# A hybrid state-space and delta-rule trunk layer on one core: the delta rule run as three side lines, state-space batches with prefetched inputs and a doubling recurrence, and the conditioning vectors loaded at other times

## The chip, the core and the metric

The kernel runs on one core of a Trainium2 chip. The metric is the time of one execution on the device in microseconds (us). Before the change the median of three runs is 3185.92 us (3182.63 to 3190.62).

## The reference, cut to what matters

One layer over 512 tokens of width 2048. A conditioning vector `c` gives six modulation vectors of 2048 entries each through the 2048 x 12288 matrix `w_ada`.

```python
mod = silu(c) @ w_ada + b_ada                       # six vectors
sh_m, sc_m, g_m, sh_f, sc_f, g_f = split(mod, 6)
h = layer_norm(x) * (1 + sc_m) + sh_m
u, q, k, v, z, beta, a, gate_s, gate_g = split(h @ w_in)
y_s = s5_mixer(u) @ w_up_ssm        # 64 groups, diagonal complex recurrence, GLU
y_g = gated_deltanet(q, k, v, z, beta, a) @ w_up_gdn      # 8 heads, chunks of 64
y = (sigmoid(gate_s) * y_s + sigmoid(gate_g) * y_g) @ w_out
x = layer_norm(ALPHA * x + g_m * y)
h = layer_norm(x) * (1 + sc_f) + sh_f
x = layer_norm(ALPHA * x + g_f * swiglu(h))
```

In the state-space mixer each group's state follows x[t] = A x[t-1] + B u[t] with a diagonal complex A. In the delta rule each head needs, for each chunk, the inverse of a unit lower triangular matrix, and then a recurrence over the chunks that updates a 128 x 128 state.

## The kernel before, in words

**The large products.** Every matrix of weights is cut into chunks of 128 x 1024 numbers (512 KB), numbered here from 0 in the order of use. Class `Weights` (L886) loads a chunk through SyncE's queue into `raw`, ScalarE copies it to `whi` (a cast to fp32r), VectorE subtracts to get the rest `wlo`, and TensorE takes both: three matmuls (`mm3`) for each 128 x 128 block. `raw`, `whi` and `wlo` have three buffers each (`NB = 3`). A chunk feeds 24 matmuls of 512 columns where the weights stand still in the array (`gemm1`, `gemm2`), but only 12 of 512 columns in the output projection (the loop over `hf` and `q` behind `ln_half`), since that runs over the weights twice, once for each half of the tokens. Chunks 0 to 17 are the projection to u and to beta and a; 18 to 145 the 16 pairs of gate columns and, for each of 8 heads, q, k, v and z; 146 to 153 the GLU; 154 to 185 the two up-projections that are merged; 186 to 249 the output projection. From 250 on it is the feed-forward network, whose first eight hidden tiles are taken over the first half of the tokens (chunks 250 to 281) and then over the second.

**Side lines.** All else is written as generators (lines) that class `Order` (L57) mixes into the matmuls when the kernel is built: it keeps an estimated clock for each engine and lets a line emit its next step where its inputs should be ready (`tick`), or, in `until`, runs lines without any large matmul between until a condition holds. The result is one fixed order for each engine, and each engine works in order.

- *State space* (`s5_setup`, `s5_batch`, `s5_line`): eight batches of eight groups. A batch loads U, B and C through SyncE, builds tables of powers on GpSimd (`powers`), does small matmuls, then runs the recurrence on VectorE as 7 steps over 64 columns and 7 steps over 8 columns (`cstep`, four operations each), a correction on GpSimd, more matmuls, GELU, and a store.
- *Delta rule* (`gdn_prep`, `gdn_solve` and the lines that call them): one line prepares head h (decays, products of keys), the other inverts the triangular blocks in five levels and runs the recurrence over four double chunks. The output of the recurrence, `po`, is held in one of the three accumulators of the large products (`psum_mm`). The preparing line starts head h when head h-2 is done.
- *Conditioning vectors* (`ada_line`, `ada_cols_line`, `ada_row_line`): each vector of 2048 is made in four parts of 512. A part is 16 loads of 128 x 512 numbers of `w_ada` (256 KB each), each scaled and added into `aacc`. Before the change these loads go through GpSimd's queue, and 5 of every 16 are scaled on ScalarE and added on GpSimd, the others on VectorE. sh_m and sc_m are made ahead of everything. The other four, 16 parts, are line `ada_rest` (L1350), added by `switch` when state space and delta rule are done.

**Who needs the vectors.** g_m is needed by the output projection (`k.ada_m`). sh_f and sc_f are needed by `ln_half`, which normalizes one half of the tokens, transposes it on TensorE (`px_tr<-cst,ld`) and writes the inputs of the feed-forward network; it waits in `while not k.ada_f`. `ln_half(0)` must be finished (`o.drain(lnl)`) before the feed-forward network starts, and `ln_half(1)` before its second half of tokens. g_f is needed behind the first group of hidden tiles (`k.ada_done`).

Of the kernel before, what the change touches and what calls it, by code (L numbers as in the profile page):

```python
# [11 lines left out]
F32 = mybir.dt.float32  # L12
# [259 lines left out]
def s5_setup(k, p, lam_re, lam_im, log_dt):  # L272
# [8 lines left out]
    s.R8s = per.tile([128, 2, 32], F32, name="R8s")  # L281
    s.R64s = per.tile([128, 2, 32], F32, name="R64s")
# [85 lines left out]
    for dst, i in ((s.R8s, 0), (s.R64s, 7)):  # L368
        e.tensor_scalar(out=dst[:, 0, :], in0=R[:, 1, i, :], scalar1=-1.0, scalar2=None, op0=M)
        e.tensor_copy(out=dst[:, 1, :], in_=R[:, 1, i, :])  # L370


def s5_batch(k, j, prm, d_col):
# [5 lines left out]
    U = t("U")  # L379
    ld.dma_start(out=U.rearrange("p (g c) -> p g c", g=8),  # L380
                 in_=k.dup[j].rearrange("(g h) (s c) -> (h s) g c", g=8, s=8))
    B = k.sm5.tile([128, 2, 8, 16], F32, name="s5B", tag="s5B")
    for half in range(2):
        for sw in range(2):
            src = (b_re, b_im)[half ^ sw]
            ld.dma_start(out=B[64 * half:64 * half + 64, sw], in_=src[0, g0:g0 + 8].rearrange("g p h -> p g h"))
    Cin = k.sm5.tile([128, 3, 64], F32, name="s5C", tag="s5C")
    for i, src in enumerate((c_re, c_im, c_re)):
        ld.dma_start(out=Cin[:, i, :], in_=src[0, g0:g0 + 8].rearrange("g h p -> (g h) p"))
# [20 lines left out]
    H = k.t5w("H").rearrange("p (g h s) -> p g h s", g=8, s=8)  # L410
# [37 lines left out]
    St = t("S").rearrange("p (q r b i) -> p q r b i", q=4, r=2, b=8)  # L448
    pSv = pS.rearrange("p (g b i) -> p g b i", g=8, b=8)
    for gp in range(2):  # L450
        for ri in range(2):
            act.copy(St[64 * gp:64 * gp + 64, :, ri].rearrange("p q b i -> p q (b i)"),
                     pSv[64 * ri:64 * ri + 64, gp::2].rearrange("p g b i -> p g (b i)"))
    yield
# [4 lines left out]
    q0 = 4 * j  # L459
    w1 = k.sm5.tile([128, 4, 2, 8], F32, name="s5w1", tag="s5w1")  # L460

    def cstep(dst, prev, rr, rs, n):
        x = w1[:, :, :, 0:n]
        shp = [128, 4, 2, n]
        for src, cf_ in ((prev, bc(rr.unsqueeze(2).unsqueeze(3), shp)), (prev[:, :, ::-1], bc(rs.rearrange("p r q -> p q r").unsqueeze(3), shp))):
            v.tensor_tensor(out=x, in0=src, in1=cf_, op=M)
            v.tensor_tensor(out=dst, in0=dst, in1=x, op=A)
    a8r, a8s = s.R8[:, 0, 0, q0:q0 + 4], s.R8s[:, :, q0:q0 + 4]
    a64r, a64s = s.R8[:, 0, 7, q0:q0 + 4], s.R64s[:, :, q0:q0 + 4]
    for i in range(1, 8):  # L470
        cstep(St[:, :, :, :, i], St[:, :, :, :, i - 1], a8r, a8s, 8)
        if i % 2 == 0:
            yield
    for b in range(1, 8):
        cstep(St[:, :, :, b, 7:8], St[:, :, :, b - 1, 7:8], a64r, a64s, 1)
        if b % 3 == 0:
            yield
    yield R
    Tp = k.t5w("K").rearrange("p (g n) -> p g n", g=8)
    act.copy(Tp.rearrange("p g (h s) -> p g s h", s=8), R.rearrange("p g (s h) -> p g s h", s=8))  # L480
    yield
    wf = k.sm5.tile([128, 4, 7, 7], F32, name="s5wf", tag="s5wf")
# [10 lines left out]
    pool.memset(X[:, :, 0:1], 0.0)  # L493
    for gp in range(2):
        for ri in range(2):
            act.copy(X[64 * ri:64 * ri + 64, gp::2, 1:64],
                     St[64 * gp:64 * gp + 64, :, ri].rearrange("p q b i -> p q (b i)")[:, :, 0:63])
    powers(H, C, slice(1, 9), S)
    yield
# [28 lines left out]
def gdn_setup(k, p, psb, a_log, dt_bias, conv_w, norm_w):  # L528
# [13 lines left out]
    s.TT = per.tile([128, 512], F32, name="TTfull")  # L542
    pool.memset(s.TT, 0.0)
# [203 lines left out]
def gdn_solve(k, h, r):  # L747

    v, act, pool, pe = k.v, k.act, k.pool, k.pe
    s, t = k.gd, k.tg  # L750
# [6 lines left out]
    def col(nm):  # L757
        return k.sm.tile([128, 4], F32, name=nm, tag="gd" + nm, bufs=2)
# [27 lines left out]
    for i in range(2):  # L786
        p = slice(64 * i, 64 * i + 64)
        v.tensor_copy(out=v4(s.TT)[p, :, p], in_=v4(TT)[p])
# [3 lines left out]
    v.tensor_scalar(out=v4(s.TT)[0:64, :, 64:128], in0=v4(px[:, 0:256])[0:64], scalar1=-1.0, scalar2=None, op0=M)  # L792
    TT = s.TT
# [19 lines left out]
    po = k.psum_mm()  # L813
    for n in T4:
        pvn = k.psum("gd")
        pe.matmul(pvn[:, 0:128], lhsT=n_(TT, n), rhs=n_(bv, n), start=True, stop=(n == 0))
        if n:
            pe.matmul(pvn[:, 0:128], lhsT=n_(wT, n), rhs=St, start=False, stop=True)
            pe.matmul(n_(po, n), lhsT=n_(r.qd, n), rhs=St, start=True, stop=False)
# [5 lines left out]
        pe.matmul(n_(po, n), lhsT=n_(r.ET, n), rhs=vn, start=(n == 0), stop=True)  # L825
# [6 lines left out]
    yield po  # L832
    so, ro = col("so"), col("ro")
    junk = t("th")
    for n in T4:
        act.activation(n_(junk, n), n_(po, n), AF.Square, accum_out=so[:, n:n + 1])
# [5 lines left out]
    on = t("th")  # L842
    v.tensor_tensor(out=v4(on), in0=v4(po), in1=c4(ro), op=M)
# [25 lines left out]
def gdn_solve_line(k):  # L869
    for h in range(8):  # L870
        while k.heads_ready <= h:
            yield 1.0
        yield from gdn_solve(k, h, k.prepped.pop(h))
# [88 lines left out]
def kernel(ctx, tc, x, c, w_ada, b_ada, w_in, lam_re, lam_im, log_dt, b_re, b_im, c_re, c_im,  # L962
# [828 lines left out]
```

## Time and profile before

| | |
|---|---|
| median of three runs | 3185.92 us |
| profiled execution, its own time | 3192.52 us |
| its span, first to last instruction | 3190.7 us |
| TensorE busy | 3039.6 us, 95% of the span |
| VectorE, ScalarE, GpSimd busy | 1649.5, 976.4, 879.7 us |
| moved from and to HBM | 458.17 MB |

The profile gives each engine's busy time, by window of time too, with the clock that TensorE was granted, the busy share of the 16 DMA engines and their GB/s. "Waits" name who waited for whom. "Groups" collect instructions by line, engine and tiles: busy us and mean ns of one, then idle time of the engine just before them and what ended it. "The chain" follows the work that ended last back from its end. Almost everything carries L170 or L211, the helpers that record an operation, so one reads by tile names; `w` is a load of `w_ada`, `s_` are state-space tiles, `g_` and `px_gd` delta-rule tiles, `at` and `bt` are activations, `pm` and `px_fo` accumulators of the large products.

### The profile page before, as it was taken

The page shows a single profiled execution, that of the slowest core. Times are in us where ns is not written, and L with a number is a line of the kernel's source. Part 1 is how long each engine was busy: PE and PEld are TensorE (multiplying, and loading weights), DVE is VectorE, ACT ScalarE, POOL GpSimd, SP SyncE. Part 2 cuts the span into 40 slices and gives each one's busy share as a digit, 9 for nine tenths or more (in the row PEclk, how much of TensorE's full clock was granted, in tenths as well). Part 3 has the DMA queues.
Part 4 walks back from the last instruction along what each step waited for, and adds up shares of the span by engine and source line. Part 5 has one row for each costly group of instructions (what it writes and reads, how often), then busy time and mean ns, then how long its engine had stood idle before and what let it go on. Part 6 is the DMA issues. An engine that isn't in the chain of part 4 may idle for free.

```text
span 3190.7 us, 40575 instructions
## 1 busy us (share of the span) xinstructions
PE 3039.6 (95%) x15953; PEld 2507.5 (79%) x15953; DVE 1649.5 (52%) x2407; ACT 976.4 (31%) x1386; POOL 879.7 (28%) x997
## 2 busy tenths in 40 slices
PE   5899999999999999998878899999999999999997
PEld 3588788888788888886758798888888888888885
DVE  6536664566545377767778653333333333333338
ACT  3233333333333244334345531221222222222121
POOL 4824434434352143333344203002001100200202
PEclk8899999999999999999989999999999999999999
DMA  9644233333333488778878463333333333333333
GB/s 339 217 126 109 72 82 92 93 88 81 84 98 86 152 283 267 235 246 290 272 232 242 137 177 108 94 99 111 94 99 108 97 99 104 101 99 97 108 106 119
DMA packets 505344, 458.17 MB, mean 144 GB/s; under 512 B 56144, under 2 KB 403632, under 8 KB 505152
## 3 DMA queue, kind: packets, MB, share of 16 engines
q1 hardware_dynamic: 477472, 375.34, 39.1%
q0 software_dynamic: 20480, 67.13, 6.2%
q10 hardware_dynamic: 7200, 13.10, 1.1%
q8 instruction: 125, 2.05, 0.3%
q14 instruction: 67, 0.55, 0.1%
HBM read 435.60 MB, written 19.89 MB: 143 GB/s over the span
## 4 chain that ended last, share of the span: by engine, by line
PE 78%; DVE 7%; DMA 6%; POOL 3%; issue 3%; ACT 2%; SPq 1%; ACTq 0%; DVEq 0%; POOLq 0%
PE pm L211 56%; PE px_fo L211 14%; PE px_gd L211 3%; DMA raw<-in_w_mix_out_dram 3%; PE px_s L211 2%; DVE wlo L170 2%; DVE at L170 1%; SPq L170 1%; DVE aacc L170 1%; ACT whi L170 1%; DMA w<-in_w_ada_dram 1%; DMA raw<-in_ffn_w_in_dram 1%; PE px_u L211 1%; POOL eq L170 1%; PE px_ada L211 0%
## 5 line engine op out<-in xcount | busy, mean ns | idle before, releaser
L211 PE MATMUL pm<-at,whi 128*128 128x512 f32 (+1 forms) x3744 | 1142.6, 388 | 7.4 <-ACT whi L170 3.6
L170 DVE TENSOR_TENSOR wlo<-raw,whi 128x1024 fp32r<-128x1024 f32 x541 | 698.4, 1293 | 773.2 <-ACT whi L170 761.3
L170 ACT CAST whi<-raw 128x1024 fp32r<-128x1024 f32 x541 | 567.0, 1049 | 1068.0 <-PE pm L211 464.8
L211 PEld LDWEIGHTS pm<-at,whi 128*128 128x128 f32 x3744 | 681.5, 190 | 138.8 <-issue 4.1
L211 PE MATMUL pm<-at,wlo 128*128 128x512 f32 (+1 forms) x1872 | 715.4, 382 | 6.4 <-DVE wlo L170 6.4
L211 PE MATMUL pm<-bt,whi 128*128 128x512 f32 (+1 forms) x2464 | 682.1, 363 | 0.7 <-ACT whi L170 0.7
L211 PEld LDWEIGHTS pm<-bt,whi 128*128 128x128 f32 x2464 | 443.9, 190 | 72.4 <-ACT whi L170 1.1
L211 PE MATMUL pm<-bt,wlo 128*128 128x512 f32 (+1 forms) x1232 | 446.9, 363 | 5.7 <-DVE wlo L170 5.7
L170 POOL TENSOR_TENSOR at<-at,ld 128x512 f32<-128x512 f32 x80 | 120.5, 1537 | 1106.9 <-DVE ld L170 1106.9
L211 PEld LDWEIGHTS pm<-at,wlo 128*128 128x128 f32 x1872 | 355.6, 190 | 76.5 <-DVE wlo L170 8.0
L211 PE MATMUL px_fo<-whi,bt 128*128 128x512 f32 x960 | 298.8, 389 | 0.0
L211 PEld LDWEIGHTS pm<-bt,wlo 128*128 128x128 f32 x1232 | 233.6, 190 | 42.6 <-DVE wlo L170 6.9
L211 PEld LDWEIGHTS px_fo<-whi,bt 128*128 128x128 f32 x960 | 180.1, 188 | 37.4
L170 POOL DMA_DIRECT2D w<-in_w_ada_dram x237 | 128.7, 544 | 291.2 <-DVE aacc L170 178.6
L211 PE MATMUL px_fo<-wlo,bt 128*128 128x512 f32 x480 | 186.7, 389 | 0.0
L170 DVE SCALAR_TENSOR_TENSOR aacc<-w,ccol,aacc 128x512 f32<-128x512 f32 x148 | 135.6, 916 | 13.4 <-DMA w<-in_w_ada_dram 11.8
L211 PE MATMUL pm<-whi,bt 128*128 128x512 f32 x336 | 112.2, 404 | 13.1 <-DVE at L170 13.0
L170 POOL TENSOR_TENSOR aacc<-aacc,w 128x512 f32<-128x512 f32 x59 | 88.2, 1495 | 77.9 <-ACT w L170 77.4
L211 PE MATMUL px_fo<-whi,at 128*128 128x512 f32 x336 | 107.5, 389 | 1.7 <-ACT whi L170 1.7
L211 PEld LDWEIGHTS px_fo<-wlo,bt 128*128 128x128 f32 x480 | 90.1, 188 | 18.7
L170 DVE SCALAR_TENSOR_TENSOR gs<-gg,pm 128x512 f32<-128x512 f32 x36 | 24.8, 688 | 142.1 <-ACT gg L170 142.1
L211 PEld LDWEIGHTS pm<-whi,bt 128*128 128x128 f32 x336 | 65.5, 195 | 30.5 <-DVE at L170 16.0
(389 smaller groups left out, 3173.6 us busy)
## 6 DMA issues: line engine op xcount, KB each, us to landing
raw<-in_ffn_w_in_dram SPq DMA_DIRECT2D x208, 512.0 KB, 4.0
raw<-in_w_in_dram SPq DMA_DIRECT2D x146, 512.0 KB, 3.7
w<-in_w_ada_dram POOLq DMA_DIRECT2D x237, 256.0 KB, 4.6
raw<-in_ffn_w_out_dram SPq DMA_DIRECT2D x88, 512.0 KB, 3.7
wad<-in_w_ada_dram SPq DMA_DIRECT2D x64, 512.0 KB, 5.8
raw<-in_w_mix_out_dram SPq DMA_DIRECT2D x64, 512.0 KB, 5.8
raw<-in_w_up_gdn_dram SPq DMA_DIRECT2D x16, 512.0 KB, 4.0
raw<-in_w_up_ssm_dram SPq DMA_DIRECT2D x16, 512.0 KB
```

The source lines that it names most:

```text
L170: r = f(*a, **kw)
L211: r = self.e.matmul(out, **kw)
```

## The change

1. **Conditioning vectors.** g_m becomes its own line, `ada_gate`, added before the state-space and delta-rule work: its 64 loads go through SyncE's queue, one in at least 6.0 us of the planner's clock (`pace`), and all adding is on VectorE. sh_f and sc_f (128 loads) stay on GpSimd's queue from `switch` on. g_f (64 loads) goes through SyncE at a pace of 3.5 us, on VectorE alone. In the order of the built programs `switch` comes ahead of chunk 118 and no longer of chunk 130. By the chunks that are split on VectorE, the sixteen parts were made from chunk 130 to 276: g_m at 130 to 152, sh_f and sc_f at 154 to 227, g_f at 229 to 276. Now g_m is made at 17 to 106, sh_f and sc_f at 118 to 157, and g_f at 159 to 245. Of g_f's four parts two, 32 loads, stand between chunks 196 and 245, inside the output projection, and none behind it.
2. **State space.** `fetch(j + 1)` loads the inputs of the next batch from the middle of batch j; U has two buffers. The powers `H` come ahead of the recurrence, the loads of `R` behind it. The recurrence is done by doubling: distances 1, 2 and 4, over 448, 384 and 256 columns and then 56, 48 and 32, four VectorE operations each, 24 in place of 56. Their tables (`s.tab`) are made in `s5_setup` by VectorE.
3. **Delta rule.** `gdn_solve` is cut into `gdn_inverse` and `gdn_recur`, each with its line, so that the inverse of head h can run beside the recurrence of head h-1. The inverse is written into `MT`. The recurrence's outputs go chunk by chunk into small accumulators (`px_go`) and are copied out by ScalarE.
4. **Places in the large products.** The pair of gate columns of a head comes between k and v and no longer ahead of q; the wait for head h-2 comes behind it.

The large products and the number of TensorE instructions in the built program (14323) stay the same.

The first place is TensorE at the end of the output projection. `px_tr<-cst,ld` are the transposes of `ln_half(0)`, `px_ada<-aacc,half` a part of g_f, `pm<-whi,...` the output projection, `pm<-bt,whi` the feed-forward network. Before:

```order
4079 L211 MATMUL pm<-wlo,bt 128x512
4080 L211 MATMUL pm<-whi,bt 128x512
4081 L216 MATMUL px_tr<-cst,ld 128x128 x12
4082 L211 MATMUL px_ada<-aacc,half 128x512
4083 L216 MATMUL px_tr<-cst,ld 128x128 x16
4084 L211 MATMUL pm<-bt,whi 128x256 x2
```

The same transposes now, from the order of the changed kernel:

```order
4066 L211 MATMUL pm<-whi,at 128x512
4067 L216 MATMUL px_tr<-cst,ld 128x128 x4
4068 L211 MATMUL pm<-whi,at 128x512
...
4074 L211 MATMUL pm<-whi,at 128x512
4075 L216 MATMUL px_tr<-cst,ld 128x128 x4
4076 L211 MATMUL pm<-whi,at 128x512
...
4082 L211 MATMUL pm<-whi,at 128x512
4083 L216 MATMUL px_tr<-cst,ld 128x128 x4
4084 L211 MATMUL pm<-whi,at 128x512
```

28 of the 32 transposes stood between the last matmul of the projection and the first of the feed-forward network; now all 32 stand inside the projection, four at a time. The 32 of `ln_half(1)`, of which 16 stood together at the boundary between the two halves of the tokens (row 4602 before), stand in eight groups of four in the same way, the last of them at the boundary (row 4611).

The second place is SyncE's queue at one state-space batch. `dz` is the store at a batch's end, `s_U`, `s5B` and `s5C` are the next batch's inputs, `Kd` a store in its middle. Before:

```order
117 L170 DMA dz_88<-s_y 128x8x64
118 L170 DMA s_U<-dup_81 128x8x64
119 L170 DMA s5B<-in_ssm_b_re_dram 64x8x16
120 L170 DMA s5B<-in_ssm_b_im_dram 64x8x16 x2
121 L170 DMA s5B<-in_ssm_b_re_dram 64x8x16
122 L170 DMA s5C<-in_ssm_c_re_dram 128x64
123 L170 DMA s5C<-in_ssm_c_im_dram 128x64
124 L170 DMA s5C<-in_ssm_c_re_dram 128x64
125 L170 DMA raw<-in_w_in_dram 128x8x128
126 L170 DMA g_G<-dG 128x512
```

Now:

```order
160 L170 DMA Kd<-s5Kc 128x240
161 L170 DMA s_U<-dup_82 128x8x64
162 L170 DMA s5B<-in_ssm_b_re_dram 64x8x16
...
167 L170 DMA s5C<-in_ssm_c_re_dram 128x64
168 L170 DMA w_5114<-in_w_ada_dram 128x512
169 L170 DMA raw<-in_w_in_dram 128x8x128 x2
170 L170 DMA w_5254<-in_w_ada_dram 128x512
171 L170 DMA s_R<-Kd 128x1x128 x8
172 L170 DMA raw<-in_w_in_dram 128x8x128
```

The inputs have moved from behind the store of the batch before to behind its `Kd`, and loads of `w_ada` for g_m now stand in this queue among the weights.

The diff, cut to its core:

```diff
 def s5_batch(k, j, prm, d_col):
+    def fetch(j):
+        ...
+        k.fetched[j] = U, B, Cin
+    if j not in k.fetched:
+        fetch(j)
+    U, B, Cin = k.fetched.pop(j)
     yield Cin
...
+    if j < 7 and k.u_done > j + 1:
+        fetch(j + 1)
+    H = k.t5w("H").rearrange("p (g h s) -> p g h s", g=8, s=8)
+    powers(H, C, slice(1, 9), S)
+    yield St
+    def level(dst, src, n, d):
+        ...
+        v.tensor_tensor(out=a, in0=src, in1=bc(re, shp), op=M)
+        v.tensor_tensor(out=b, in0=src[:, ::-1], in1=bc(sg, shp), op=M)
+        v.tensor_tensor(out=dst, in0=dst, in1=a, op=A)
+        v.tensor_tensor(out=dst, in0=dst, in1=b, op=A)
+    for d in (1, 2, 4):
+        level(St[:, :, :, :, d:8], St[:, :, :, :, 0:8 - d], 8, d)
+        yield
+    for d in (1, 2, 4):
+        level(St[:, :, :, d:8, 7], St[:, :, :, 0:8 - d, 7], 64, d)
+    yield H
     R = k.t5w("R").rearrange("p (g n) -> p g n", g=8)
...
-    for i in range(1, 8):
-        cstep(St[:, :, :, :, i], St[:, :, :, :, i - 1], a8r, a8s, 8)
-    for b in range(1, 8):
-        cstep(St[:, :, :, b, 7:8], St[:, :, :, b - 1, 7:8], a64r, a64s, 1)
...
-    powers(H, C, slice(1, 9), S)
```

```diff
+def gdn_recur(k, h, r):
...
-    po = k.psum_mm()
+    def output(n, ps):
+        act.activation(n_(junk, n), ps, AF.Square, accum_out=so[:, n:n + 1])
+        act.copy(n_(bv, n), ps)
     for n in T4:
         pvn = k.psum("gd")
+        pon = k.psum("go")[:, 0:128]
...
+def gdn_recur_line(k):
+    for h in range(8):
+        while k.heads_inverted <= h:
+            yield 1.0
+        yield from gdn_recur(k, h, k.prepped.pop(h))
         k.heads_done = h + 1
```

```diff
-    def ada_line(p, col0):
+    def ada_line(p, col0, pace):
...
-        acc2 = P2[1].tile([128, 512], F32, name="aacc2", tag="aacc2", bufs=1) if P2 else None
+        acc2 = None if pace else P2[1].tile([128, 512], F32, name="aacc2", tag="aacc2", bufs=1)
-        depth = 6 if k.ada_deep else 4
+        deep = k.ada_deep and not pace
+        depth = 3 if pace else 6 if deep else 4
+        eng = k.sync if pace else pool
...
-            pool.dma_start(out=raw, in_=w_ada[0, k0:k0 + 128, col0:col0 + 512])
+            eng.dma_start(out=raw, in_=w_ada[0, k0:k0 + 128, col0:col0 + 512])
...
             yield raws[kt]
-            while not P2 and o.free["v"] > o.clock + 0.2:
+            if pace:
+                yield pace
+            while pace and not P2 and o.free["v"] > o.clock + 0.2:
                 yield 0.7
...
+    def ada_gate():
+        for q in range(4):
+            yield from ada_row_line(adp, 2, q, 6.0)
+        k.ada_m = True
     def ada_rest():
-        for q in range(4):
-            yield from ada_row_line(adp, 2, q)
-        k.ada_m = True
+        while not k.ada_m:
+            yield 2.0
...
-            yield from ada_row_line(adp, 5, q)
+            yield from ada_row_line(adp, 5, q, 3.5)
         k.ada_done = True
+    o.add(ada_gate())
...
     for h in range(8):
-        for j in itertools.islice(gate_next, GATES_BEFORE[h]):
-            gemm2(16, hT, gate_out(j))
-        o.until(lambda: k.heads_done >= h - 1)
+        o.until(lambda: k.heads_ready >= h - 1)
         for b in range(3):
+            if b == 2:
+                for j in itertools.islice(gate_next, GATES_BEFORE[h]):
+                    gemm2(16, hT, gate_out(j))
+                o.until(lambda: k.heads_done >= h - 1)
             ps = gemm1(hT)
```

More of the change, by code (lines that the diff above doesn't have):

```diff
@@ L280, in s5_setup @@
     s.R8 = per.tile([128, 2, 8, 32], F32, name="R8")
-    s.R8s = per.tile([128, 2, 32], F32, name="R8s")
-    s.R64s = per.tile([128, 2, 32], F32, name="R64s")
+    s.tab = {(n, d, x): per.tile([128, 8, 2, 4], F32, name=f"tab{n}{d}{x}") for n in (8, 64) for d in (1, 2, 4) for x in "rs"}
     s.E16 = per.tile([128, 16], F32, name="E16")
@@ L378, in s5_batch @@
     g0 = 8 * j
[L379 to L389, printed above, removed]
+    def fetch(j):
+        g0 = 8 * j
+        U = t("U")
+        ld.dma_start(out=U.rearrange("p (g c) -> p g c", g=8),
+                     in_=k.dup[j].rearrange("(g h) (s c) -> (h s) g c", g=8, s=8))
+        B = k.sm5.tile([128, 2, 8, 16], F32, name="s5B", tag="s5B")
+        for half in range(2):
+            for sw in range(2):
+                src = (b_re, b_im)[half ^ sw]
+                ld.dma_start(out=B[64 * half:64 * half + 64, sw], in_=src[0, g0:g0 + 8].rearrange("g p h -> p g h"))
+        Cin = k.sm5.tile([128, 3, 64], F32, name="s5C", tag="s5C")
+        for i, src in enumerate((c_re, c_im, c_re)):
+            ld.dma_start(out=Cin[:, i, :], in_=src[0, g0:g0 + 8].rearrange("g h p -> (g h) p"))
+        k.fetched[j] = U, B, Cin
+    if j not in k.fetched:
+        fetch(j)
+    U, B, Cin = k.fetched.pop(j)
     yield Cin
@@ L791, in gdn_solve, with col @@
         pe.matmul(b_(px, n, 0), lhsT=b_(X, n, 1), rhs=b_(TT, n, 1), start=True, stop=True)
-    v.tensor_scalar(out=v4(s.TT)[0:64, :, 64:128], in0=v4(px[:, 0:256])[0:64], scalar1=-1.0, scalar2=None, op0=M)
-    TT = s.TT
+    v.tensor_scalar(out=v4(MT)[0:64, :, 64:128], in0=v4(px[:, 0:256])[0:64], scalar1=-1.0, scalar2=None, op0=M)
+def gdn_recur(k, h, r):
+    v, act, pool, pe = k.v, k.act, k.pool, k.pe
+    s, t = k.gd, k.tg
+    T4 = range(4)
+    def col(nm):
+        return k.sm.tile([128, 4], F32, name=nm, tag="gd" + nm, bufs=2)
+    TT = r.MT
     while (h, 2) not in k.heads:
@@ L831, in gdn_solve @@
             yield St
[L832 to L836, printed above, removed]
+        else:
+            yield pon
+        output(n, pon)
     yield so
@@ L841, in gdn_solve @@
     yield ro
[L842 to L843 removed]
+    on = bv
+    v.tensor_tensor(out=v4(on), in0=v4(bv), in1=c4(ro), op=M)
     while (h, 3) not in k.heads:
```

110 lines of the change are left out of this document (60 added, 50 removed).

## The prediction

> **What bounds the kernel now.** I read the page's slices first: the row of TensorE, the clock granted to it, the share of the DMA engines and their GB/s.
>
> ```profile
> PE   5899999999999999998878899999999999999997
> PEclk8899999999999999999989999999999999999999
> DMA  9644233333333488778878463333333333333333
> GB/s 339 217 126 109 72 82 92 93 88 81 84 98 86 152 283 267 235 246 290 272 232 242 137 177 108 94 99 111 94 99 108 97 99 104 101 99 97 108 106 119
> ```
>
> A slice is 80 us. TensorE works nearly all the time; counted from 0, it is below 9 in the first slices and again from slice 18 to 22 (8, 8, 7, 8, 8), where the clock also drops once. From slice 14 to 21 the DMA engines carry 230 to 290 GB/s, against 72 to 98 from slice 4 to 12. So the DMA load is uneven, and TensorE lags at the end of its high part. I then cut the span at the stages (300 to 1083: state space and delta rule; to 1431: the remaining gates, GLU and merge; to 1656: output projection; to 1682: the hole behind it; to 1786 and 1814: the first half of the first feed-forward group and the wait at its end).
>
> ```profile
> core 0: us, PE busy (x) PEld busy (x) DVE busy (x) ACT busy (x) POOL busy (x), PEclk, DMA share, GB/s
> 300.00:1083.00 783.00, 765.13 (x5384) 636.61 (x5384) 437.93 (x975) 248.18 (x472) 304.85 (x313) 0.98 0.32 87
> 1083.00:1431.00 348.00, 348.00 (x1546) 287.21 (x1545) 242.11 (x282) 134.03 (x169) 130.19 (x182) 1.00 0.78 255
> 1431.00:1656.00 225.00, 198.37 (x808) 154.82 (x807) 174.38 (x210) 88.70 (x100) 81.81 (x104) 0.94 0.84 273
> 1656.00:1682.00 26.00, 9.29 (x33) 5.75 (x32) 14.98 (x29) 16.24 (x32) 17.05 (x20) 0.58 0.57 179
> 1682.00:1786.00 104.00, 93.65 (x725) 90.23 (x725) 87.65 (x114) 47.61 (x66) 44.31 (x46) 0.97 0.74 220
> 1786.00:1814.00 28.00, 18.28 (x121) 16.96 (x120) 13.00 (x24) 23.25 (x44) 9.29 (x7) 0.82 0.23 66
> ```
>
> Busy flatters TensorE, whose matmuls overlap. The chain shows undisturbed stretches of the same matmuls: 768 of 512 columns, and 768 of 256.
>
> ```profile
> 1988.81 174.08 PE pm L211 x768
> 1808.89 92.84 PE pm L211 x768
> ```
>
> The output projection is 64 chunks of 12 matmuls, 768 of 512 columns, and takes 225 us in place of 174. The half group behind it is 768 of 256 columns and takes 104 + 28 us in place of 93. With the 26 us of the hole that is 51 + 26 + 39 = 116 us lost between 1431 and 1814. From 1083 to 1431 nothing is lost. From 300 to 1083 TensorE stands idle for 783 - 765 = 18 us.
>
> What ends those waits: the groups, transfers and waits of the output projection.
>
> ```profile
> L170 DVE TENSOR_TENSOR wlo<-raw,whi 128x1024 fp32r<-128x1024 f32 x64 | 84.6, 1331 | 46.3 <-ACT whi L170 46.3
> L170 ACT CAST whi<-raw 128x1024 fp32r<-128x1024 f32 x64 | 66.9, 1047 | 123.5 <-DMA raw<-in_w_mix_out_dram 90.9 <-PE pm L211 30.3 <-issue 1.6
> L170 DVE SCALAR_TENSOR_TENSOR aacc<-w,ccol,aacc 128x512 f32<-128x512 f32 x47 | 40.4, 861 | 0.8 <-DMA w<-in_w_ada_dram 0.5
> ...
> DMA packets 30806, 61.41 MB, mean 273 GB/s; under 512 B 2718, under 2 KB 6597, under 8 KB 30793
> raw<-in_w_mix_out_dram SPq DMA_DIRECT2D x59, 512.0 KB, 5.8
> w<-in_w_ada_dram POOLq DMA_DIRECT2D x74, 256.0 KB, 5.6
> ```
>
> ScalarE waits 90.9 us for weights, VectorE then for ScalarE, TensorE for VectorE: the stage is held by transfers, and 74 of them, 74 x 0.262 = 19.4 of 61.4 MB, are `w_ada`. In the hole the waits name TensorE waiting for ScalarE's `ld`, the input of the transposes; the two groups below them are the transposes' and VectorE's products there.
>
> ```profile
> PE px_tr L216 <- ACT ld L170: 12.8, 6, 6.9
> PE px_ada L211 <- DVE aacc L170: 3.9, 1, 3.9
> ...
> L216 PE MATMUL px_tr<-cst,ld 128*128 128x128 f32 x28 | 7.3, 411 | 12.8 <-ACT ld L170 12.8
> L170 DVE SCALAR_TENSOR_TENSOR aacc<-w,ccol,aacc 128x512 f32<-128x512 f32 x6 | 5.1, 851 | 1.2 <-DMA w<-in_w_ada_dram 1.1
> ```
>
> **The output projection: 225 to 190, -35.** The order leaves 32 loads of `w_ada` there in place of 74. That takes away 42 x 0.262 = 11.0 MB and leaves 50.4 MB, 185 us at the 273 GB/s reached now. TensorE needs 174 plus 7 for the transposes that move in, 181. VectorE has 174 us of work now; 32 products in place of 47 take 15 x 0.861 = 13 away, and the work of `ln_half(0)` in the hole, 15.0 less 5.1 of `aacc`, comes in: 171. Three limits at 171 to 185 with three buffers between them will not overlap perfectly; I take 190. Bounds: 181 (TensorE alone), and 221 if VectorE reaches no more than its present share (174.4 of 225, 77.5%; 171 / 0.775).
>
> **The hole: 26 to 3, -23.** sh_f and sc_f are complete by chunk 157, so `ln_half(0)` no longer waits for them, and all its transposes stand inside the projection. Bounds 0 and 10: ScalarE and GpSimd may run behind the order.
>
> **The half group: 104 to 95, and its end: 28 to 8, together -29.** The two rows stand for these 132 us.
>
> ```profile
> w<-in_w_ada_dram POOLq DMA_DIRECT2D x24, 256.0 KB, 4.7
> PE px_tr L216 <- ACT ld L170: 9.7, 6, 3.9
> ```
>
> The 24 loads and their adding are gone, and the same weights with no `w_ada` beside them flow at 93 us (the chain's second row); with transposes 95, bounds 93 and 104. At the end 16 transposes of `ln_half(1)` stood in a row, each group waiting for ScalarE; now four stand there. I take 8; bounds 2 and 20.
>
> **State space and delta rule: -8.** These are all the waits of TensorE from 300 to 1083 that the view of waits names with over 1 us.
>
> ```profile
> PE px_s L216 <- DMA s5C<-in_ssm_c_im_dram: 8.5, 6, 2.7
> PE px_gd L211 <- ACT g_th L170: 4.4, 1, 4.4
> PE px_gd L216 <- DVE g_th L170: 3.5, 2, 1.8
> ```
>
> Prefetching removes the first, 8.5: the inputs are issued in the middle of the batch before. The other two lie at the head's recurrence and may go or come back; all three together, 16.4, are the most that three lines and doubling can bring, since the work of TensorE is unchanged. What the edits do to VectorE is worked out from these rows and the `aacc` row above.
>
> ```profile
> L170 DVE TENSOR_TENSOR s_S<-s_S,s5w 128x64 f32<-128x64 f32 x98 | 28.9, 295 | 3.4
> L170 DVE TENSOR_TENSOR s_S<-s_S,s5w 128x8 f32<-128x8 f32 x98 | 23.4, 238 | 3.4
> L170 DVE TENSOR_TENSOR s5w<-s_S,R8s 128x64 f32<-128x64 f32 x49 | 14.3, 293 | 1.7
> L170 DVE TENSOR_TENSOR s5w<-s_S,R64s 128x8 f32<-128x8 f32 x49 | 9.3, 190 | 1.7
> L170 DVE TENSOR_TENSOR pm<-pm,grow 128x512 f32<-128x512 f32 x16 | 11.0, 688 | 0.0
> ```
>
> A batch's recurrence is now 14 operations of each of the four kinds (one stands for its equals), 14 x (0.295 + 0.238 + 0.293 + 0.190) = 14.2 us. Doubling has 12 wide operations of 256 to 448 columns, between the rows of 64 and of 512 columns: by the straight line 0.42 to 0.63, 6.3 us, and 12 short ones like those of 8 to 64, some 3. That is 5 us less a batch, 40 in all, off TensorE's path. g_m adds 64 x 0.861 = 55 us to VectorE there. 438 - 40 + 55 = 453 us of 783, 58% for 56%: VectorE does not become the bound. The loads of g_m are 17 MB more in a stage at 87 GB/s, hidden. On SyncE they stand among the weights, so a load that waits for its buffer would hold a weight back; with three of four buffers loaded ahead and 6.0 us between them none should. `R` now waits in that queue for GpSimd's `H`, with the next weights behind it; a chunk lasts 24 x 0.227 = 5.4 us and three are in flight, 16 us of cover. The copies by ScalarE of the recurrence's outputs (32 of 128 columns, ScalarE busy 248 of 783) lie beside TensorE work: nothing. I take -8, bounds -16 and +10.
>
> **Gates, GLU and merge: +3.** sh_f and sc_f now follow each other without a gap: 128 loads, 33.6 MB, over 39 chunks (118 to 157), 39 x 5.44 = 212 us, 0.158 MB a us.
>
> ```profile
> 1083.00:1209.00 126.00, 126.00 (x553) 103.19 (x552) 81.19 (x92) 54.20 (x67) 46.96 (x68) 1.00 0.80 265
> w<-in_w_ada_dram POOLq DMA_DIRECT2D x38, 256.0 KB, 4.8
> gg<-in_w_ada_dram POOLq DMA_DIRECT2D x18, 256.0 KB, 5.0
> ```
>
> Before, 56 loads came in 126 us, 0.117 a us, at a total of 265 GB/s and with TensorE never idle. 41 GB/s more make 306 at a share near 0.92. I expect a few late products, +3; bounds 0 and +25 (306 GB/s against the 273 that the output projection reaches, 12% of 212). The start gets a few more small table operations, the rest of the feed-forward network and the end are not touched: 0.
>
> **The sum.** -35 - 23 - 29 - 8 + 3 = -92 us against the profiled execution's own 3192.5, 3100.5. The median of the runs shown is 3185.92, 0.2% below that execution, so 3100.5 x 3185.92 / 3192.52 = 3094.
>
> **Rivals.** *The projection keeps its own limit* (its three-buffer ring: transfer, cast and subtraction in a row for each chunk of only 2.7 us of matmuls). For it: VectorE still needs 171 of 181 us. Against it: a weight lands there in 5.8 us (the row above) and in 4.0 in the second half of the group, where no `w_ada` flows.
>
> ```profile
> raw<-in_ffn_w_in_dram SPq DMA_DIRECT2D x26, 512.0 KB, 4.0
> ```
>
> In that case the stage stays at 221: +31, 3125. *The DMA bound moves ahead* to chunks 118 to 157: for it the 306 GB/s above, against it that no TensorE wait of any size stands between 1083 and 1431 now. +25 in place of +3: 3116. *VectorE and GpSimd get into each other's way* in the first half of the state space, the one that ends slower.
>
> ```profile
> 1438.89 1.22 DVE wlo L170
> ...
> L170 DVE TENSOR_TENSOR wlo<-raw,whi 128x1024 fp32r<-128x1024 f32 x1 | 3.0, 3015 | 0.0
> L170 POOL TENSOR_TENSOR s_W<-PAi,s5bb 128x1024 f32<-128x1024 f32 x1 | 3.0, 2999 | 0.0
> ```
>
> A subtraction of 1.22 us took 3.02 when it started beside GpSimd's product of tables (826 to 832 us). The 96 wide doubling steps (12 in each of 8 batches) are VectorE operations on two SBUF inputs, and the powers `H` of the same batch now stand directly ahead of them on GpSimd. 96 x 1.8 = 173 us of VectorE, and if all of it reached TensorE 3094 + 173 = 3267; it ends slower than before from 53% of that on. Against it: GpSimd is busy 305 of 783 us, VectorE would still be at 80%, and TensorE has matmuls of other lines between. The Trainium skill, page "SBUF — State Buffer", section "Who interferes with whom", has the rule: a VectorE instruction with two SBUF inputs and a GpSimd instruction that reads SBUF exclude each other for a whole instruction. By that rule every such meeting costs up to the length of the GpSimd operation; the two rows agree, 3.02 beside 3.00.
>
> **How the numbers follow.** The forecast's own case has 0.70, the projection's limit 0.13, the DMA bound ahead 0.10, the collision 0.07. The first three are all faster than before by over 0.3%, about what a measurement of this kernel can tell from no change; of the last I count 0.05 as slower and 0.02 as within 0.3%: 0.93, 0.02, 0.05. If every term meets its better bound (-44, -26, -11, -26, -16, 0: -123) the time is 3063, and the range begins there. Upwards it takes in both middle rivals together, 3094 + 31 + 22 = 3147.
>
> **What would show it right or wrong.** Right: from the first matmul of the output projection to the second half of the group about 296 us in place of 383, with no idle stretch of over 5 us between projection and feed-forward network; the clock there near 1; `s5C` gone from TensorE's waits; the first stage some 8 us shorter. Wrong: whi still waiting over 60 us for `w_mix_out`, TensorE idle between chunks 118 and 157, or the state-space stage longer than before with wide `s_S` operations of well over 0.7 us.

## The result and the profile after

The changed kernel takes 3167.82 us, median of 4 runs (3164.91 to 3170.39), against 3188.27 of before (3182.63 to 3190.71, 4 runs): ratio 0.9938, 95% interval 0.9919 to 0.9957. It is faster by 20 us, and the interval is clear of 1. The forecast was 3094 us with a range from 3063 to 3147: the direction is right, the size is not.

The profiled execution took 3170.34 us, its span is 3168.6. The slices of the changed kernel, to be laid beside those of before:

```profile
PE   5899989989999999999989999999999999999997
PEclk8899989999999999999999999999999999999998
DMA  9654334333332688656866553333333333333333
GB/s 330 229 148 110 98 87 111 105 105 95 117 109 84 201 288 288 224 188 207 261 225 192 169 170 103 100 97 110 94 99 110 97 100 101 105 95 102 109 101 120
```

Counted from 0, the dip of TensorE in slices 18 to 22 is gone but for an 8 in slice 20, and so is the one of its clock in slice 20. New are 8s of TensorE in slices 5 and 8, in the state-space stage.

The same work in both kernels is best cut by the chunks of weights, each stage from the start of VectorE's subtraction (`wlo`) of one chunk to that of another: 18 to 154, to 186, to 250 and to 298 (state space, delta rule and gates; GLU and merge; output projection; half group and its end). These are the windows of before, with the columns shown in the prediction:

```profile
210.40:1244.40 1034.00, 1014.49 (x6510) 842.56 (x6509) 602.86 (x1203) 352.66 (x611) 396.25 (x427) 0.99 0.40 116
1244.40:1421.30 176.90, 176.90 (x798) 147.05 (x797) 129.54 (x154) 60.05 (x75) 66.15 (x89) 1.00 0.77 248
1421.30:1652.00 230.70, 204.07 (x836) 159.67 (x835) 176.31 (x212) 88.71 (x101) 83.06 (x106) 0.94 0.83 273
1652.00:1851.30 199.30, 162.52 (x1200) 153.41 (x1199) 138.51 (x192) 104.40 (x163) 72.90 (x73) 0.90 0.63 187
```

and these the windows of the changed kernel:

```profile
211.90:1284.90 1073.00, 1032.19 (x6568) 853.68 (x6567) 693.14 (x1056) 367.84 (x661) 470.86 (x494) 0.97 0.46 139
1284.90:1459.50 174.60, 174.60 (x774) 144.31 (x773) 110.20 (x139) 46.43 (x55) 4.64 (x6) 1.00 0.61 201
1459.50:1680.40 220.90, 198.41 (x837) 156.80 (x836) 155.62 (x204) 89.93 (x109) 27.61 (x18) 0.96 0.72 231
1680.40:1828.30 147.90, 143.80 (x1163) 141.51 (x1163) 98.47 (x136) 79.79 (x118) 26.38 (x18) 0.99 0.65 183
```

The last stage became 51 us shorter, the projection 10, and the first one 39 us longer: TensorE stands idle there for 1073 - 1032 = 41 us in place of 20, and its mean clock falls from 0.99 to 0.97. Who it waits for there, in the changed kernel:

```profile
PE px_ada L211 <- DVE aacc L170: 7.3, 2, 4.6
PE px_s L216 <- POOL s_V L170: 6.7, 4, 3.8
PE px_gd L216 <- DVE g_v L170: 5.9, 2, 5.2
PE px_gd L211 <- ACT g_th L170: 4.0, 1, 4.0
PE px_gd L211 <- DVE St L170: 2.8, 1, 2.8
PE px_gd L211 <- DVE g_T L170: 2.8, 2, 1.7
PE px_gd L211 <- POOL g_T L170: 2.3, 2, 2.1
...
```

`s5C` has gone, as forecast. In its place stand many waits of a few us each, spread over the side lines' matmuls, for VectorE, GpSimd and ScalarE; none is for weights.

The projection's transfers still hold ScalarE up, but less, and it waits more for a buffer that TensorE has to free. The groups of the changed kernel between 1459 and 1680 us:

```profile
L170 DVE TENSOR_TENSOR wlo<-raw,whi 128x1024 fp32r<-128x1024 f32 x64 | 78.1, 1228 | 52.7 <-ACT whi L170 52.4
L170 ACT CAST whi<-raw 128x1024 fp32r<-128x1024 f32 x65 | 68.2, 1050 | 116.4 <-DMA raw<-in_w_mix_out_dram 69.2 <-PE pm L211 43.0 <-DVE wlo L170 1.9
```

### The profile page after: what moved, and what is told of

Same layout as the page of the kernel before. It is cut to its first block, busy times and chain, and to the rows that moved or that the text cites. A ratio compares the mean times of both kernels' runs of the same rounds, so it can differ in the third digit from the quotient of the medians.

```text
span 3168.6 us, 40305 instructions
## 1 busy us (share of the span) xinstructions
PE 3033.4 (96%) x15953; PEld 2499.7 (79%) x15953; DVE 1663.2 (52%) x2217; ACT 954.5 (30%) x1378; POOL 782.8 (25%) x832
## 4 chain that ended last, share of the span: by engine, by line
PE 64%; DMA 4%; DVE 4%; issue 2%; ACT 2%; POOL 1%; SPq 0%; ACTq 0%; DVEq 0%; POOLq 0%
PE pm L211 47%; PE px_fo L211 14%; DMA raw<-in_w_mix_out_dram 2%; PE px_gd L211 2%; DVE wlo L170 1%; ACT whi L170 1%; DVE at L170 1%; DMA w<-in_w_ada_dram 1%; DVE aacc L170 1%; PE px_ada L211 0%; DMA raw<-in_ffn_w_in_dram 0%; PE px_s L211 0%; ACT f L170 0%; DVE bt L170 0%; DMA g_G<-dG 0%
## 5 line engine op out<-in xcount | busy, mean ns | idle before, releaser
L170 DVE TENSOR_TENSOR wlo<-raw,whi 128x1024 fp32r<-128x1024 f32 x541 | 683.4, 1265 | 800.6 <-ACT whi L170 789.7
L170 ACT CAST whi<-raw 128x1024 fp32r<-128x1024 f32 x541 | 567.0, 1050 | 1066.4 <-PE pm L211 454.9
L170 DVE SCALAR_TENSOR_TENSOR aacc<-w,ccol,aacc 128x512 f32<-128x512 f32 x176 | 163.8, 931 | 6.1 <-DMA w<-in_w_ada_dram 5.1
L170 POOL TENSOR_TENSOR rs<-rs,mhalf 128x1 f32<-128x1 f32 (+1 forms) x13 | 11.3, 872 | 453.1 <-DVE rs L170 453.1
L211 PEld LDWEIGHTS px_fo<-wlo,bt 128*128 128x128 f32 x480 | 90.1, 188 | 18.7
L170 DVE TENSOR_TENSOR gs<-gs,pm 128x512 f32<-128x512 f32 x36 | 24.7, 687 | 119.9 <-PE pm L211 119.9
L211 PEld LDWEIGHTS pm<-whi,bt 128*128 128x128 f32 x336 | 64.9, 193 | 26.4 <-DVE at L170 11.7
```

Source lines behind the costliest of these rows:

```text
L170: r = f(*a, **kw)
L211: r = self.e.matmul(out, **kw)
```

## The experiments

Fourteen kernels, all run in three rounds and profiled. "Stage" is chunk 18 to 154, "idle" the sum of TensorE's gaps of over 0.25 us in it, "half" the time in it with a granted clock of 0.5; "projection" is chunk 186 to 250, "group" 250 to 298; all in us and from one profile of each kernel. The time is the median.

| kernel | time | stage | idle | half | projection | group |
|---|---|---|---|---|---|---|
| before | 3188.3 | 1034.0 | 18.7 | 23.9 | 230.7 | 199.3 |
| changed | 3167.8 | 1073.0 | 40.0 | 54.6 | 220.9 | 147.9 |
| changed, batches of before | 3154.1 | 1057.8 | 33.5 | 30.7 | 208.9 | 161.6 |
| changed, one solving line | 3158.7 | 1062.4 | 32.5 | 41.0 | 221.1 | 146.6 |
| changed, g_m late | 3155.8 | 1046.1 | 27.5 | 34.1 | 215.7 | 155.5 |
| changed, batches spaced | 3149.2 | 1056.1 | 30.9 | 30.7 | 207.7 | 152.8 |
| before with new vectors | 3159.8 | 1070.0 | 40.8 | 51.2 | 207.1 | 156.7 |
| changed, loads left out | 3159.1 | 1076.2 | 47.7 | 44.4 | 204.1 | 147.7 |
| changed, products cut | 3148.7 | 1069.5 | 40.1 | 41.0 | 201.9 | 146.4 |
| spaced and g_m late | 3159.3 | 1051.9 | 30.4 | 30.7 | 216.1 | 157.0 |
| changed, margin 1.2 | 3121.3 | 1016.9 | 9.0 | 3.4 | 200.1 | 173.1 |
| before, margin 1.2 | 3255.2 | 1093.3 | 67.8 | 64.9 | 215.6 | 216.8 |
| spaced, margin 0.8 | 3142.7 | 1050.5 | 27.6 | 34.1 | 211.7 | 153.8 |
| changed, margin 1.2 to the switch | 3112.6 | 1018.7 | 9.0 | 6.8 | 212.8 | 152.7 |
| one line, margin 1.2 | 3216.0 | 1115.0 | 82.6 | 99.0 | 208.3 | 163.0 |
| batches of before, margin 1.2 | 3149.3 | 1015.0 | 9.1 | 6.8 | 207.7 | 173.8 |

One sum holds in the table. Stage less idle less half of "half" is 1002 to 1010 us in every kernel but the two with long stops (before and one line, both with margin 1.2): 1034 - 19 - 12 = 1003, 1073 - 40 - 27 = 1006. Of the 39 us, 21 are waits and 15 the half clock that follows them; the 2 left are within the spread of the sum, so the work itself is the same. 37 of the 40 us of idle time lie ahead of chunk 118. In the projection the same sum gives 187 to 193 in all sixteen.

**Which part of the change brings the waits.** Four kernels, each with one part undone. The batches of before (`s5_setup` and `s5_batch` whole, with their buffers):

```diff
-    for d in (1, 2, 4):
-        level(St[:, :, :, :, d:8], St[:, :, :, :, 0:8 - d], 8, d)
...
+    for i in range(1, 8):
+        cstep(St[:, :, :, :, i], St[:, :, :, :, i - 1], a8r, a8s, 8)
...
```

> The changed kernel with the state-space batches of before (recurrence in steps of one, inputs loaded at the batch's start, H behind the recurrence); three delta-rule lines, gate places and early vectors stay. Its order puts the ends of the eight batches at chunks 34, 45, 56, 67, 78, 90, 101, 113 in place of 30 to 80. The measure is the stage from VectorE's subtraction of chunk 18 to that of chunk 154: 1033.9 us before, 1073.1 in the changed kernel. Density theory (batches that follow each other a third faster make VectorE and GpSimd run behind, TensorE waits and then gets half clock): the stage comes down to 1030 to 1045, with half clock again near 24 us in all from chunk 18 to 118; total 3135 to 3150. Lines theory (inverse and recurrence beside each other cost it): 1065 to 1075, total 3165 to 3180. Gate-vector theory (64 loads and products of g_m in the stage cost it): 1065 to 1075 as well.

Inverse and recurrence in one line:

```diff
         yield from gdn_inverse(k, k.prepped[h])
-        k.heads_inverted = h + 1
+        yield from gdn_recur(k, h, k.prepped.pop(h))
+        k.heads_done = h + 1
...
-    o.add(gdn_inverse_line(k))
-    gl = o.add(gdn_recur_line(k))
+    gl = o.add(gdn_inverse_line(k))
```

> The changed kernel with inverse and recurrence of the delta rule one behind the other in one line again; all else stays. Lines theory: the stage from chunk 18 to 154 falls from 1073 to 1030 to 1045, total near 3140. Density theory and gate-vector theory: the stage stays at 1060 to 1075, total 3160 to 3175; the eight batches still end between chunks 30 and 85.

g_m behind the switch, through GpSimd's queue again and with its products shared among three engines as before:

```diff
-    def ada_gate():
+    def ada_rest():
         for q in range(4):
-            yield from ada_row_line(adp, 2, q, 6.0)
+            yield from ada_row_line(adp, 2, q, 0)
         k.ada_m = True
-    def ada_rest():
-        while not k.ada_m:
-            yield 2.0
...
-    o.add(ada_gate())
```

> The changed kernel with g_m not made early but as before, through GpSimd's queue behind the switch, ahead of sh_f and sc_f; all else stays. Gate-vector theory: the stage from chunk 18 to 118 (816 us before, 864 in the changed kernel) falls to about 820 to 830. Density theory and lines theory: it stays at 850 to 870, since 55 us of VectorE spread over 760 us are not what TensorE waits for. Behind chunk 154 the vectors come later again (sh_f and sc_f up to chunk 186, g_f up to 290): there I expect 10 to 30 us lost against the changed kernel under every theory, so the total says little, 3170 to 3200.

Batches spaced:

```diff
-        while k.u_done <= j:
+        while k.u_done <= j or (j and (j, 0) not in k.heads):
```

> The changed kernel with one condition more: batch j of the state space starts only once q of head j is out of the large products. The batches keep doubling, prefetch and the early H, but end at chunks 30, 39, 49, 63, 74, 86, 99, 111 in place of 30, 39, 44, 51, 58, 66, 73, 80. Density theory: the stage from chunk 18 to 154 falls from 1073 to 1030 to 1050 and the half clock to 25 to 30 us in all, total 3130 to 3155. Theory that the doubling steps themselves collide with GpSimd's powers: the stage stays at 1060 to 1075, and wide steps of the recurrence of over 1 us are as many as in the changed kernel. Lines and gate-vector theories: 1060 to 1075.

All four are misses in part. Each edit gives something of the stage back, 15, 11, 27 and 17 us, 70 together where 39 had been lost, and none reaches the 1034 of before. The 11 and 15 are weak: the four runs of the one-line kernel alone lie 10 us apart. g_m late is the largest; from chunk 18 to 118 it brings 864 us to 844, between what the gate-vector theory (820 to 830) and the other two (850 to 870) had named. Then both of the strongest at once, and the counterpart, the kernel of before with only the new vectors (its `ada_line`, `ada_gate` and `ada_rest` are those of the changed kernel):

```diff
     def ada_rest():
-        for q in range(4):
-            yield from ada_row_line(adp, 2, q)
-        k.ada_m = True
+        while not k.ada_m:
+            yield 2.0
...
+    o.add(ada_gate())
```

> The changed kernel with both edits that helped: batch j of the state space waits for q of head j, and g_m is made behind the switch through GpSimd's queue, as before. If both take away the same thing (VectorE and GpSimd behind their order), the stage from chunk 18 to 154 goes no lower than 1035 to 1046 and the total is 3140 to 3155. If they are separate losses that add up (27 and 17 us), the stage is 1025 to 1035 and the total 3125 to 3140.

> The kernel of before with only the conditioning vectors of the changed kernel: g_m early through SyncE with its products on VectorE, sh_f and sc_f behind the switch, g_f at a pace of 3.5 us. State space and delta rule are as before, eight batches at one per head. Theory that g_m's 64 products cost the stage in any case: from chunk 18 to 154 it takes 1050 to 1060 us (1034 before plus 16 to 27). Theory that they cost only where the batches follow each other densely: 1034 to 1042. Behind chunk 154 both say about what the changed kernel has, so the total is 3145 to 3160 by the first and 3125 to 3145 by the second.

With both edits the stage is 1052, no better than with g_m late alone: they do not add up. The vectors alone lengthen the stage of before from 1034 to 1070, more than the first theory's 27 us, with a batch per head as ever; density is not needed for the loss. All its idle time, 41 us for 19, lies ahead of chunk 118, where g_m is the only one of the four late vectors that is made. Window of before with the new vectors, first stage:

```profile
208.90:1278.90 1070.00, 1027.89 (x6542) 850.13 (x6541) 672.23 (x1268) 352.80 (x611) 410.98 (x425) 0.98 0.43 126
```

**Loads or products of the vectors.** Loads left out:

```diff
+            if pace and raws:
+                raws.append(raws[0])
+                return
             n = k.ada_n = k.ada_n + 1
```

> The changed kernel with the loads of g_m and g_f left out: of each part's sixteen loads only the first is made, and all sixteen products read it, so both vectors are not what the reference asks for; VectorE has the same products. State-space stage (chunk 18 to 154, 1073 us): if the loads among the weights in SyncE's queue cost it, 1045 to 1055; if VectorE's products cost it, 1065 to 1075. Output projection (chunk 186 to 250, 221 us): if the share of the transfers sets it, as the forecast had it, 8 MB less at 231 GB/s make it 185 to 195; if its own ring of three buffers and VectorE's order set it, 205 to 220.

Products cut:

```diff
+                w = 8 if pace else 512
-                v.scalar_tensor_tensor(out=acc, in0=raws[kt], scalar=sc, in1=acc, op0=M, op1=A)
+                v.scalar_tensor_tensor(out=acc[:, 0:w], in0=raws[kt][:, 0:w], scalar=sc, in1=acc[:, 0:w], op0=M, op1=A)
```

> The changed kernel with all loads, but with the products of g_m and g_f cut from 512 to 8 columns (all but the first of each part), so both vectors are not what the reference asks for. State-space stage (1073 us): if VectorE's time in the products costs it, 1045 to 1055; if the loads do, 1065 to 1075. Output projection (221 us): if the transfers set it, 215 to 222; if VectorE's order sets it, 30 products of 0.80 us less make it 197 to 210.

In the stage neither edit alone helps: 1076 and 1070. The loads are hidden, as the forecast had it. Cutting the products to a 64th of their size frees VectorE of less than half their time: ahead of chunk 118 the products of g_m take 35 us in place of 63. The groups of the changed kernel and of this one (chunk 18 to 154, where the first line takes in 50 products of sh_f and sc_f; mean ns behind the busy us):

```profile
L170 DVE SCALAR_TENSOR_TENSOR aacc<-w,ccol,aacc 128x512 f32<-128x512 f32 x111 | 111.5, 1005 | 5.9 <-DMA w<-in_w_ada_dram 5.1
...
L170 DVE TENSOR_TENSOR s_S<-s_S,s_K 128x448 f32<-128x448 f32 x16 | 14.0, 872 | 0.6
...
L170 DVE TENSOR_TENSOR s_K<-s_S,tab81s 128x448 f32<-128x448 f32 x8 | 11.7, 1460 | 0.0
...
L170 DVE TENSOR_TENSOR s_K<-s_S,tab81r 128x448 f32<-128x448 f32 x8 | 10.7, 1337 | 0.5 <-ACT s_S L170 0.5
```

```profile
L170 DVE SCALAR_TENSOR_TENSOR aacc<-w,ccol,aacc 128x8 f32<-128x8 f32 x59 | 33.4, 566 | 0.0
```

The small products still take 0.566 us each in the mean, with a median of 0.222. A stretch of the timeline shows why some are long (start, length). The changed kernel:

```profile
587.71 2.38 POOL L170 TENSOR_TENSOR s_V<-s_V,s_W 128x1024 f32<-128x1024 f32 x1
...
587.82 0.41 DVE L170 TENSOR_TENSOR g_TT<-g_TT,px_gd 128x256 f32<-128x256 f32 x1
...
588.15 2.50 DVE L170 SCALAR_TENSOR_TENSOR aacc<-w,ccol,aacc 128x512 f32<-128x512 f32 x1
```

and the one with cut products:

```profile
580.03 3.43 POOL L170 TENSOR_TENSOR s_V<-s_V,s_W 128x1024 f32<-128x1024 f32 x1
...
581.12 0.42 DVE L170 TENSOR_TENSOR g_X<-px_gd,cmix 128x256 f32<-128x256 f32 x1
...
581.46 2.03 DVE L170 SCALAR_TENSOR_TENSOR aacc<-w,ccol,aacc 128x8 f32<-128x8 f32 x1
```

A product that starts while GpSimd runs a product of tables ends behind it: 588.15 + 2.50 = 590.65 against 587.71 + 2.38 = 590.09, and 583.49 against 583.46. VectorE's operations with one input in PSUM in between (`px_gd`, 0.41 and 0.42 us) are not held up. The Trainium skill, page "SBUF — State Buffer", section "Who interferes with whom", says that a VectorE instruction with two SBUF inputs contends with a GpSimd instruction that reads SBUF. The trace agrees, with 2.03 us for 8 columns. The planner reckons 0.2 + 512 x 0.00105 = 0.74 us for a product of 512 columns, which is the median measured, and has no term for a wait on GpSimd.

In the projection both edits help alike, 204 and 202 for 221. But three kernels take 207 to 209 with all loads and products of g_f in place (old batches, spaced, vectors alone). They make 37 to 39 loads of `w_ada` there for the 32 of the changed kernel, and move 51 to 52 MB at 246 to 252 GB/s for its 51 MB at 231: it is not the transfers that hold it at 221.

**The order's margin.** What all these kernels share is the planner's clock: a side line emits a step 0.4 us (`MARGIN`) after its inputs should be ready, and TensorE stands if they are late.

```diff
-    MARGIN = 0.4
+    MARGIN = 1.2
```

> The changed kernel with one number of the planner changed: a side line may emit its next step 1.2 us, no longer 0.4, after its inputs should be ready. Nothing is computed otherwise. Theory that TensorE waits because VectorE, held up beside GpSimd, is later than the planner's clock by about a microsecond at a time: TensorE's gaps from chunk 18 to 154 fall from 40 us to under 20, half clock from 55 to under 30, the stage from 1073 to 1020 to 1045, total 3120 to 3150 (the vectors come some chunks later). Rival that VectorE is behind by far more than a microsecond, a backlog that a margin can't cover: the stage stays at 1060 to 1075.

The stage falls to 1017 us, below the forecast's own value and 17 us below that of before, and the kernel takes 3121.26 us, ratio 0.9785 (0.9771 to 0.9800). Window and TensorE's largest waits of this kernel, the latter up to chunk 118; behind it there are none:

```profile
211.60:1228.50 1016.90, 1007.01 (x6550) 838.68 (x6549) 662.67 (x1026) 359.85 (x649) 436.65 (x450) 1.00 0.46 138
```

```profile
PE px_gd L211 <- DVE St L170: 2.8, 1, 2.8
PE px_gd L211 <- DVE g_X L170: 2.0, 1, 2.0
PE px_gd L211 <- DVE g_T L170: 1.3, 1, 1.3
PE px_s L216 <- POOL s_V L170: 1.2, 3, 0.7
...
```

VectorE's products are hardly shorter, 0.99 us in the mean for 1.01:

```profile
L170 DVE SCALAR_TENSOR_TENSOR aacc<-w,ccol,aacc 128x512 f32<-128x512 f32 x95 | 94.1, 990 | 0.7
...
L170 DVE TENSOR_TENSOR s_K<-s_S,tab81s 128x448 f32<-128x448 f32 x8 | 9.8, 1228 | 0.0
```

So the collisions and g_m's products are still there (57 of the 61 ahead of chunk 118); what has gone is most of TensorE's waiting, 9 us idle for 40. Two more with a margin:

> The kernel of before with the same number, 1.2 in place of 0.4. By the first theory its 18.7 us of gaps and 23.9 us of half clock from chunk 18 to 154 shrink as well: the stage goes from 1034 to 1012 to 1030. But state space and delta rule end later, and all sixteen parts of the vectors with them, so the tail behind chunk 186 gets longer by 5 to 20 us; total 3175 to 3195. By the rival the stage stays at 1030 to 1040 and the total is 3190 to 3210.

> The changed kernel with the batches spaced by the heads, as in the earlier run, and 0.8 us in place of 0.4 in the planner. By the first theory the stage from chunk 18 to 154 falls from the 1056 us of the spaced kernel to 1025 to 1045 and the total from 3149 to 3115 to 3138. By the rival 1050 to 1060 and 3145 to 3155.

Both are misses. 0.8 us with spaced batches is not enough: 27.6 us idle, stage 1050, which is what the rival of a backlog had named. 1.2 us with spaced batches was not run, so where between 0.8 and 1.2 the waits go is open. And the kernel of before gets 65 us slower, ratio 1.0204 (1.0187 to 1.0221). Ahead of chunk 118 its idle time goes from 19 to 24 us, 18 of them waits for `s5C`; most of the loss comes behind. Its waits between chunks 118 and 154:

```profile
PE px_ada L211 <- DVE aacc L170: 44.3, 2, 24.2
```

Its delta rule now stores its last head at chunk 138 in place of 125 (at 122 in the changed kernel with 1.2). The switch comes so late, near chunk 142, that the inputs of the GLU (chunk 146) and the vectors are made with hardly a large product left to run beside them. Which part of the change keeps the other kernel from that, and where its own remaining loss lies, the last three kernels test. The first has `o.MARGIN = 0.4` in `switch`, the others are the one-line and the old-batches kernels with 1.2.

> The changed kernel with 1.2 us of margin up to the switch and 0.4 from there on, so that sh_f, sc_f and g_f come earlier again (g_f up to chunk 264 in place of 284). If the 25 us that the kernel with 1.2 us throughout lost against the changed one between chunk 250 and 298 (173 us for 148) come from the later vectors, that stretch falls to 145 to 160 and the total from 3121 to 3095 to 3113, with the stage again at 1010 to 1025. If they come from something else, the stretch stays at 165 to 175 and the total at 3115 to 3127.

> The changed kernel with 1.2 us throughout, and with inverse and recurrence in one line. Theory that a margin needs room, which the three lines give: the delta rule of one line takes longer than the large products beside it, the switch comes at chunk 144 in place of 128, TensorE has gaps of over 25 us between chunks 118 and 154 as the kernel of before had with this margin (44 us there), and the total is 3150 to 3200. Rival, that the doubling and the prefetch give the room: the stage stays at 1015 to 1030 and the total at 3120 to 3135.

> The changed kernel with 1.2 us throughout, and with the state-space batches of before. Theory that the three lines alone give the room: no gaps of over 10 us between chunks 118 and 154, the stage at 1010 to 1035, the vectors later still (g_f up to chunk 316), total 3120 to 3150. Rival, that doubling and prefetch are needed: gaps of over 25 us between 118 and 154, stage over 1050, total over 3160.

With the margin up to the switch only, the group falls from 173 to 153 us as forecast, the projection is 213, and the kernel takes 3112.62 us, ratio 0.9767 (0.9753 to 0.9782): 74 us faster than before and the fastest of all. Up to the switch its order is that of the kernel with 1.2 throughout, and the stages of the two differ by 2 us. With one line the switch is late again (last head at chunk 138), chunk 118 to 154 takes 267 us, 40 us of it idle, and the kernel is slower than before (ratio 1.0089, 1.0072 to 1.0106) and than the 3150 to 3200 expected: another 43 us are idle ahead of chunk 118, 32 of them waits for `g_v`. With the old batches and three lines the last head comes at chunk 126 and the stage is 1015 us: the lines give the room, doubling and prefetch are not needed for it. Its total is 3149, since g_f comes so late (its last part at chunk 315) that 27 us are idle behind chunk 298.

## Why the prediction was wrong

By its terms, from the profiles, in us:

| term | forecast | measured |
|---|---|---|
| start, up to chunk 18 | 0 | +1.6 |
| state space, delta rule, gates (18 to 154) | -8 and part of +3 | +39.0 |
| GLU and merge (154 to 186) | rest of +3 | -2.3 |
| output projection (186 to 250) | -35 | -9.8 |
| hole, half group and its end (250 to 298) | -23 and -29 | -51.4 |
| behind it | 0 | +0.8 |
| sum | -92 | -22.1 |

**The step that failed: "State space and delta rule: -8."** It took the waits that TensorE had, 16.4 us, as the stake, and argued from shares of busy time that VectorE "does not become the bound". 58% was forecast for 300 to 1083; over the same chunks (300 to 1124) 517 of 824 us, 63%, were measured. Both are far from full, and that was the wrong question. TensorE's order holds some 3300 small matmuls of the side lines in this stage, each placed 0.4 us behind the moment at which the planner believes its input ready. A step of VectorE or GpSimd that ends later than that makes TensorE wait, and half clock often follows. So 39 us were lost in place of the 8 gained, 21 of waits and 15 of half clock. With a margin of 1.2 us nearly all of it is gone, while VectorE's busy time goes only from 693 to 663 us.

That the stage itself could become shorter was right: 17 us with the margin. That is slightly more than the 16.4 that the forecast called the most, because it left the half clock out: 23.9 us in the kernel before, 3.4 with the margin. One reading is off besides: the straight line between the two rows gives 0.46 us at 256 columns, not 0.42, which makes 6.7 us of the 6.3 for a batch and changes nothing.

**The collision rival** had the mechanism and not its place. The 16 widest multiplications take 1.34 to 1.46 us for the 0.63 forecast, but all 96 wide steps together only 69 us for 50. The g_m products, which the rival left out, are held up as well: 61 of them take 63 us ahead of chunk 118, 17 more than at their median. It priced VectorE's time; with the margin that time falls by a few per cent and three quarters of TensorE's waits go. Whether the collisions are what made the steps late was not tested by themselves.

**The output projection: 225 to 190.** Mis-sized: 221. The signs named for that came true, whi waits 69.2 us for `w_mix_out`. 51 MB were moved at 231 GB/s and not at 273, and other kernels moved as much in less time, so the transfers no longer set the stage. 190 is what is left in every kernel without waits and half clock (187 to 193). That it equals the forecast is luck: the forecast put TensorE's own work at 181 and gave 9 us to imperfect overlap, and the changed kernel has 22 us idle and 17 us of half clock on top of 190. Its waits are these:

```profile
PE pm L211 <- DVE at L170: 9.8, 5, 4.1
PE pm L211 <- DVE wlo L170: 5.5, 7, 1.0
PE px_ada L211 <- DVE aacc L170: 4.8, 1, 4.8
```

`at` is VectorE's eviction of an accumulator, behind which the next of three cannot start. The rival that kept the stage at 221 has the number, and names the ring of buffers as a limit of its own; the same ring took 208 us with as many transfers in three other kernels, so it is no fixed limit. Why kernels with nearly the same work there take 200 to 221 us stays open. The margin may play a part here too, since the stage took 200 us with 1.2 throughout and 213 with 0.4 from the switch on; but the vectors then come at other chunks as well.

**Right:** hole and half group (-51 for -52), no idle stretch of over 5 us between the projection and the feed-forward network, `s5C` gone, the loads of g_m hidden, no wait between chunks 154 and 186 and 2.7 us between 118 and 154 (the rival of the DMA bound ahead did not occur), next to nothing at the start and the end.

**Open:** whether g_m's products or only its places in the order make TensorE late at 0.4 us of margin. Leaving out the loads gave nothing and cutting the products 3 us; making the whole later gave 27 us. The parts of the change do not add up, so how the 39 us divide among them is not shown.

## What to carry to other kernels

In this kernel, whose order is fixed when it is built, the share of busy time of a helping engine said little. So look for what stands in TensorE's order with how much slack (time between an input's readiness and the place of the step that needs it), and count each new instruction on a helper as possible lateness for what stands behind it. Slack needs room: splitting a serial line so that its stages overlap brought nothing by itself here (the last head is stored at chunk 115 with one line and with three), but it let every step be placed later. So try the margin again after each such change, and forecast an added load by what it does to the waits, not to the sums.

## What the runs showed of the hardware

Half clock follows gaps that are short. These are TensorE's gaps in chunk 18 to 154 over the sixteen profiles, those alone that start 7 us or more from any other gap of over 0.3 us. A stretch of half clock (mostly 3.4 or 6.8 us) began within 7 us behind 2 of 55 of 0.3 to 1 us, 5 of 36 of 1 to 1.5 us, 19 of 35 of 1.5 to 2 us, 30 of 43 of 2 to 3 us, and 34 of 35 of 3 to 14 us. As an estimate from these counts (49 of 78 between 1.5 and 3 us, and half of the stretch lost), a single wait of 2 us costs some 3 to 4. The Trainium skill, page "TensorE: Matmul & The Clock Gate", in its part on the clock gate, names an idle window of about 3.4 us. Here half of that is often enough.

A VectorE product of two SBUF inputs that started beside a GpSimd product of tables ended behind it in both sizes shown: by 0.03 us with 8 columns and by 0.56 us with 512. In the mean the products of 8 columns took 0.34 us more than their median of 0.22 us, and those of 512 columns ahead of chunk 118 0.28 us more than theirs of 0.74.
